# Six pairs of split-weight tiles, 13 ring tiles, and a selection made a block ahead of its gather

## The chip, the cores and the metric

One NeuronCore of a Trainium2 chip runs the whole program. The metric is the device time of one execution in microseconds (us). Engines: TensorE (PE: matmuls; PEld: its weight loads), VectorE (DVE), ScalarE (ACT), GpSimd (POOL), SyncE (SP, which issues nearly all the loads here).

## What is computed

Two layers of a decoder trunk for 256 tokens of width 1024, in float32. The change touches only the last part, the mixture of experts of the second layer; its reference is

```python
def moe_swiglu(t, router, w_gate, w_up, w_down):
    logits = (t @ router).astype(jnp.float32)
    top_logits, top_idx = lax.top_k(logits, TOP_K)          # 2 of 8 experts
    gates = jax.nn.softmax(top_logits, axis=-1)
    combine = jnp.sum(jax.nn.one_hot(top_idx, N_EXPERTS, dtype=jnp.float32) * gates[..., None], axis=1)
    out = jnp.zeros_like(t)
    for e in range(N_EXPERTS):
        out = out + combine[:, e:e + 1].astype(t.dtype) * swiglu(t, w_gate[e], w_up[e], w_down[e])
    return out
```

with `swiglu` = `(silu(t @ w_gate) * (t @ w_up)) @ w_down` and experts 3584 wide. All eight experts' weights, 352 MB, are read once. A final RMSNorm follows.

## The kernel before, in words

**Turns.** The experts are worked off in eight turns (`experts`, line 1360). After routing, the experts are ranked by their count of tokens, and `KIND` alternates a large turn ("L", up to 128 tokens) with a small one ("S", up to 64 tokens). Which expert a turn takes is known only on the chip; SP loads its number into a register (`turns`, lines 1353 to 1355) and addresses the weights with it.

**Pieces.** A turn has seven blocks of 512 hidden columns. A block has eight gate/up pieces (`gate_up`) and four down pieces (`down`); a piece is a 128 x 1024 slab of float32 weights. In program order the gate/up pieces of block fc + 1 come before the down pieces of block fc. Each piece is split into two float32r tiles, high and low (`split_to`): ScalarE copies the slab into the high part, VectorE subtracts it to get the low part, and TensorE multiplies with both. A large turn needs six matmuls per piece (the tokens are split as well), a small one four: the high and low halves of its 64 tokens stand beside each other in one 128-wide operand.

**The hidden tile.** A large turn's product of silu and up is transposed and split in `hidden_T`. A small turn's is folded from its two halves by matmuls, goes through silu, product and split in `fold`, and these steps are put off by a count of pieces (`after`, counted down by `tick` after each piece).

**The selection and the gather** (`dispatch`, line 1387). For the next turn, `pick` compares the slot numbers with the ranks on VectorE (tile `sel`, two comparisons); TensorE gathers the tokens with `sel` as an operand (tile `xT`), transposes `sel` for the later combine, and `split_to` writes the gathered tokens to the tile `x`, one buffer shared by all turns. `dispatch` is a generator, advanced twice per down piece in the fifth block (fc = 4, lines 1639 to 1643), and once per down piece in the sixth. `combine` adds a turn's output to `h` during the next turn.

**Buffers and order.** Raw weights land in a ring of 16 tiles of 1 MB (`ring`: four `wraw0`, seven `wraw2`, three pairs of `wraw`, two `a8p`). There are four pairs of split tiles (`whl`, three; `whl2`, one), and `run_ahead` (line 1482) splits `AHEAD` = 3 pieces beyond the one in use. From line 1717 on, TensorE, ScalarE and VectorE keep the order in which the program issues (`in_order`); SP's loads are ordered by the planner, each as soon as its ring tile is free. Ahead of the experts, `NRAW2` = 7 loads go to `wraw2` at once (line 1609), and one more is issued by GpSimd.

Of the kernel before, what the change touches and what calls it, by code (L numbers as in the profile page):

```python
# [11 lines left out]
F32R = mybir.dt.float32r  # L12
# [17 lines left out]
CDEC = -math.exp(-0.5)  # L30
NEG = -1.0e30
NWRAW = 6
NRAW2 = 7
NRAW0 = 4
AHEAD = 3
PRE = 2


# [72 lines left out]
def _build(tc, nc, es, I, out, dbg, upto):  # L111
# [1248 lines left out]
    def experts(kinds, late=None, hook=None):  # L1360
# [26 lines left out]
        def dispatch(e, late=None):  # L1387

            large = kinds[e] == "L"
            sel = mt.tile([128, 2, 128], F32, name="sel", bufs=1)  # L1390
            rk = col(e, 0)

            def pick(tb):
                if large:
                    nc.vector.tensor_scalar(sel[:, tb, :], iota, rk(tb), None, op0=OP.is_equal)
                else:
                    nc.vector.tensor_scalar(sel[:, tb, :].rearrange("p (a b) -> p a b", a=2),
                                            iota[:, None, 0:64].to_broadcast([128, 2, 64]), rk(tb), None,
                                            op0=OP.is_equal)

            def gather(q, k, tb):
                c = slice((4 * q + k) * 128, (4 * q + k + 1) * 128)
                nc.tensor.matmul(pts[q][:, k, :], lhsT=N.t[tb][:, c], rhs=sel[:, tb, :],
                                 start=tb == 0 and (k == 0 or late is None), stop=tb == 1 and (k == 3 or late is None))
            pts = {}

            def parts(q):
                if q == 0:
                    X[e] = mo.tile([128, 2, 8, 128], F32R, name="x")
                split_to(X[e][:, 0, 4 * q:4 * q + 4], X[e][:, 1, 4 * q:4 * q + 4], pts[q])  # L1410

            def turned():
                pt = ps([128, 2, 128], "selT")
                for tb in range(2):
                    nc.tensor.transpose(pt[:, tb, :], sel[:, tb, :], ident)
                yield
                sT = SEL[e] = mt.tile([128, 2, 128], F32R, name="sT")
                nc.scalar.copy(out=sT, in_=pt)
                yield
            pick(0)  # L1420
            if late is None:
                pick(1)
            yield
            if not large:
                pt = ps([128, 8, 64], "xT")
                for kb in range(8):
                    for tb in range(2):
                        nc.tensor.matmul(pt[:, kb, :], lhsT=N.t[tb][:, kb * 128:(kb + 1) * 128], rhs=sel[:, tb, 0:64],  # L1428
                                         start=tb == 0, stop=tb == 1)
                    if kb % 2:  # L1430
                        yield
                yield from turned()
                yield "parts"
                for _ in range(2):
                    yield
                X[e] = mo.tile([128, 2, 8, 128], F32R, name="x")[:, 0]
                split_to(X[e][:, :, 0:64], X[e][:, :, 64:128], pt)
            else:
                if late is not None:
                    next(late)  # L1440
                    for q in range(2):
                        pts[q] = ps([128, 4, 128], "xT")
                        for k in range(4):
                            gather(q, k, 0)
                            if (q, k) == (1, 1):
                                next(late)
                    pick(1)
                    next(late, None)
                for q in range(2):
                    if late is None:  # L1450
                        pts[q] = ps([128, 4, 128], "xT")
                    for k in range(4):
                        if late is None:
                            gather(q, k, 0)
                        gather(q, k, 1)
                        if k % 2:
                            yield
                    if late is not None:
                        parts(q)
                yield from turned()  # L1460
                if late is None:
                    yield "parts"
                    for q in range(2):
                        yield
                        parts(q)
# [38 lines left out]
        def gate_up(e, fc):  # L1504
            large = kinds[e] == "L"
            acc = []
            sums = {}
            for w in range(2):
                a = ps([128, 512], "gu", "gu")
                for i in range(4):  # L1510
                    wh, wl = piece()
                    terms = []
                    for k in range(2):
                        kb = 2 * i + k
                        c = slice(k * 512, (k + 1) * 512)
                        x = (X[e][:, 0, kb, :], X[e][:, 1, kb, :]) if large else X[e][:, kb, :]
                        terms.append((a, x, (wh[:, c], wl[:, c]), kb == 0, kb == 7))
                    products(large, terms)
                    tick()
                    next(side[0], None)  # L1520
                acc.append(a)
                if not large:
                    t = sums[w] = mt.tile([128, 512], F32, name=("msg", "mhl")[w], **({} if w else {"bufs": 1}))
                    after(1 if (e, fc) == (last, NFC - 1) else 3, lambda t=t, a=a: nc.scalar.copy(out=t, in_=a))
            end = (e, fc) == (last, NFC - 1)
            if not large:
                return fold(sums, end)
            sgt = mt.tile([128, 512], F32, name="msg", bufs=1)
            nc.scalar.activation(sgt, acc[0], AF.Silu)
            if end:  # L1530
                preload(AF.Sqrt)
            nc.vector.tensor_tensor(out=sgt, in0=sgt, in1=acc[1], op=OP.mult)
            return sgt

        def fold(sums, end):

            H = mt.tile([128, 4, 128], F32R, name="mhh")
            t = mt.tile([128, 512], F32, name="mhl").rearrange("p (w f t) -> p w f t", w=2, f=4)
            pt = []

            def turned(w, fs):
                if not pt:
                    pt.append(ps([128, 2, 4, 64], "hT", "hT"))
                for f in fs:
                    nc.tensor.matmul(pt[0][:, w, f, :], lhsT=sums[w][:, f * 128:(f + 1) * 128], rhs=C("fold"),  # L1545
                                     start=True, stop=True)

            def silu():
                nc.scalar.activation(t[:, 0], pt[0][:, 0], AF.Silu)

            def times():
                nc.vector.tensor_tensor(out=t[:, 1], in0=t[:, 0], in1=pt[0][:, 1], op=OP.mult)  # L1552

            def parts():
                split_to(H[:, :, 0:64], H[:, :, 64:128], t[:, 1])
            for i in range(4):
                after(2 if end else 2 + i, lambda i=i: turned(i // 2, range(2 * (i % 2), 2 * (i % 2) + 2)))
            for n, f in zip((2, 2, 2) if end else (7, 8, 10), (silu, times, parts)):
                after(n, f)
            if end:  # L1560
                after(5, lambda: preload(AF.Sqrt))
            return H
# [67 lines left out]
        for e in range(len(kinds)):  # L1630
            Y = [ps([128, 512], "Y", "Y") for _ in range(2)]
            for fc in range(NFC):
                if fc + 1 < NFC:
                    nx = gate_up(e, fc + 1)
                elif e < last:
                    nx = gate_up(e + 1, 0)
                else:
                    nx = None
                if fc == NFC - 3 and e < last:
                    nxt = dispatch(e + 1)  # L1640
                    side[0] = until_parts(nxt)
                    hd = down(e, fc, hd, Y, nx, 2)
                    run(side[0])
                elif fc == NFC - 2 and e < last:
                    side[0] = nxt
                    hd = down(e, fc, hd, Y, nx, 1)
                    run(nxt)
                else:
                    hd = down(e, fc, hd, Y, nx)
                if (e, fc) == (0, 1) and hook is not None:  # L1650
                    side[0] = hook()
            side[0] = combine(e, Y, 3 if e < last else 0)
# [4 lines left out]
    last = 99  # L1657
# [33 lines left out]
    mt = left(es, "moet", 2)  # L1691
    mo = left(es, "moe", 1)
    ring[:0] = [wraw] * (NWRAW // 2) + [a8p]
    parts_.append(left(es, "whl2", 1))
    dump("h3", h)
    if upto <= 3:
        return
# [108 lines left out]
```

## Time and profile before

| | us |
|---|---|
| median of 3 runs | 1521.27 (1520.98 to 1522.26) |
| profiled execution | 1520.23 |
| its span, first to last instruction | 1518.2 |
| TensorE matmuls busy | 1439.5 (95%) |
| VectorE busy | 1244.5 (82%) |
| ScalarE busy | 1047.0 (69%) |
| mean granted TensorE clock, share of full | 0.987 |

Busy times are summed over the whole span, and the two layers' other parts take the first 550 us or so; what an engine does in the turns has to be read from stretches within them. Matmuls are pipelined and their ends are modelled, so the time from one start to the next says more than a matmul's duration. A gather matmul of the program appears as two matmuls in the trace.

### The profile page before, as it was taken

The page shows a single profiled execution, that of the slowest core. Times are in us where ns is not written, and L with a number is a line of the kernel's source. Part 1 is how long each engine was busy: PE and PEld are TensorE (multiplying, and loading weights), DVE is VectorE, ACT ScalarE, POOL GpSimd, SP SyncE. Part 2 cuts the span into 40 slices and gives each one's busy share as a digit, 9 for nine tenths or more (in the row PEclk, how much of TensorE's full clock was granted, in tenths as well). Part 3 has the DMA queues.
Part 4 walks back from the last instruction along what each step waited for, and adds up shares of the span by engine and source line. Part 5 has one row for each costly group of instructions (what it writes and reads, how often), then busy time and mean ns, then how long its engine had stood idle before and what let it go on. Part 6 is the DMA issues. An engine that isn't in the chain of part 4 may idle for free. (4 is left out here: it accounts for less than half of the span.)

```text
span 1518.2 us, 22487 instructions
## 1 busy us (share of the span) xinstructions
PE 1439.5 (95%) x7781; PEld 1206.6 (79%) x7781; DVE 1244.5 (82%) x1634; ACT 1047.0 (69%) x1440; POOL 85.9 (6%) x154
## 2 busy tenths in 40 slices
PE   7889899999999999999989999989999989999995
PEld 6879888998888888787678887777888678878774
DVE  6786865554486669989989989989989989998996
ACT  6644345444454567879878769878768879777895
POOL 4223010001020010000000000000000000000000
PEclk9999999999999999999999999999999999999998
DMA  8230025557554659889999989999999999998961
GB/s 301 73 103 24 1 85 185 187 182 268 192 180 140 262 187 380 333 341 388 400 371 400 355 334 382 404 381 389 367 358 341 400 417 358 374 368 330 389 270 46
DMA packets 78994, 426.85 MB, mean 281 GB/s; under 512 B 9280, under 2 KB 9552, under 8 KB 43920
## 3 DMA queue, kind: packets, MB, share of 16 engines
q1 hardware_dynamic: 78048, 422.38, 73.9%
q0 software_dynamic: 816, 2.87, 0.6%
q8 instruction: 65, 1.06, 0.3%
q14 instruction: 65, 0.53, 0.1%
HBM read 424.15 MB, written 1.05 MB: 280 GB/s over the span
## 5 line engine op out<-in xcount | busy, mean ns | idle before, releaser
L193 DVE TENSOR_TENSOR wlo<-mraw,whi 128x1024 fp32r<-128x1024 f32 x546 | 645.1, 1220 | 48.3 <-ACT whi L192 39.9
L192 ACT CAST whi<-mraw 128x1024 fp32r<-128x1024 f32 x546 | 559.9, 1050 | 118.5 <-PE Y L1500 57.3
L1500 PE MATMUL gu<-whi,x 128*128 128x512 f32 x1344 | 388.1, 397 | 0.1
L193 DVE TENSOR_TENSOR wlo<-raw,whi 128x1024 fp32r<-128x1024 f32 x242 | 291.3, 1220 | 108.1 <-ACT whi L192 105.6
L192 ACT CAST whi<-raw 128x1024 fp32r<-128x1024 f32 x242 | 250.1, 1043 | 132.7 <-PE acc L197 37.9
L1500 PEld LDWEIGHTS gu<-whi,x 128*128 128x128 f32 x1344 | 248.3, 188 | 52.6 <-DVE x L193 0.4
L1502 PE MATMUL gu<-wlo,x 128*128 128x512 f32 x896 | 282.6, 397 | 3.7 <-DVE wlo L193 2.8
L1502 PEld LDWEIGHTS gu<-wlo,x 128*128 128x128 f32 x896 | 165.0, 188 | 53.3 <-DVE wlo L193 17.9
L1500 PE MATMUL Y<-whi,mhh 128*128 128x512 f32 x448 | 171.3, 422 | 18.2 <-DVE mhh L193 17.8
L1502 PE MATMUL Y<-wlo,mhh 128*128 128x512 f32 x448 | 141.9, 398 | 0.7
L1500 PEld LDWEIGHTS Y<-whi,mhh 128*128 128x128 f32 x448 | 79.2, 190 | 41.1 <-DVE mhh L193 28.7
L1502 PEld LDWEIGHTS Y<-wlo,mhh 128*128 128x128 f32 x448 | 84.0, 190 | 24.0 <-DVE wlo L193 4.9
L196 PE MATMUL cp<-u,whi 128*128 128x256 f32 (+1 forms) x360 | 101.9, 283 | 0.0
L197 PE MATMUL cp<-u,wlo 128*128 128x256 f32 (+1 forms) x360 | 101.8, 283 | 0.0
L198 PE MATMUL cp<-u,whi 128*128 128x256 f32 (+1 forms) x360 | 101.8, 283 | 0.0
L1500 PE MATMUL Y<-whi,mhl 128*128 128x512 f32 x224 | 88.0, 393 | 0.0
L197 PEld LDWEIGHTS cp<-u,wlo 128*128 128x128 f32 (+1 forms) x360 | 68.3, 190 | 0.3
L196 PEld LDWEIGHTS cp<-u,whi 128*128 128x128 f32 (+1 forms) x360 | 68.3, 190 | 0.3
L198 PEld LDWEIGHTS cp<-u,whi 128*128 128x128 f32 (+1 forms) x360 | 68.3, 190 | 0.2
L1500 PEld LDWEIGHTS Y<-whi,mhl 128*128 128x128 f32 x224 | 42.2, 188 | 7.9
L196 PE MATMUL tp<-whi,u 128*128 128x512 f32 x96 | 40.8, 425 | 2.4 <-DVE u L193 2.4
L197 PE MATMUL tp<-whi,u 128*128 128x512 f32 x96 | 39.5, 412 | 2.2 <-DVE u L193 2.2
(425 smaller groups left out, 1985.1 us busy)
## 6 DMA issues: line engine op xcount, KB each, us to landing
mraw<-in_moe SPq DMA_DIRECT2D x272, 1024.0 KB, 7.2
raw<-in_moe SPq DMA_DIRECT2D x126, 512.0 KB, 7.5
raw<-in_ffn_gu SPq DMA_DIRECT2D x44, 512.0 KB, 4.0
raw<-in_w_in SPq DMA_DIRECT2D x38, 512.0 KB, 3.9
raw<-in_ffn_d SPq DMA_DIRECT2D x22, 512.0 KB, 3.6
raw<-in_w_out SPq DMA_DIRECT2D x16, 512.0 KB, 3.6
raw<-in_w_in SPq DMA_DIRECT2D x4, 416.0 KB, 8.9
h<-in_x SPq DMA_DIRECT2D x2, 512.0 KB, 6.2
```

The source lines that it names most:

```text
L192: nc.scalar.copy(out=hi, in_=src)
L193: nc.vector.tensor_tensor(out=lo, in0=src, in1=hi.bitcast(F32), op=OP.subtract)
L196: nc.tensor.matmul(o, lhsT=a[0], rhs=b[0], start=start, stop=False)
L197: nc.tensor.matmul(o, lhsT=a[1], rhs=b[0], start=False, stop=False)
L198: nc.tensor.matmul(o, lhsT=a[0], rhs=b[1], start=False, stop=stop)
L1500: nc.tensor.matmul(o, lhsT=x, rhs=b[0], start=start and i == 0, stop=False)
L1502: nc.tensor.matmul(o, lhsT=a[0] if large else a, rhs=b[1], start=False, stop=stop)
```

## The change

Six pairs of split tiles instead of four (`whl2` has three, and stands three times in the list of pools that the splits take in turn), and `AHEAD` is 5. `wraw2` has four tiles instead of seven, so the ring has 13. A small turn's gathered tokens get a tile of their own, `xs`, of half the size. In `experts`, `dispatch` of the next turn is begun, and its selection made, right after the down pieces of the fourth block; the rest follows in the fifth as before, and its last steps (the split of the gathered tokens) run in the gate/up pieces issued next. The counts by which `fold` and the copies of a small turn's sums are put off fall by two, except in the last block.

```diff
-NRAW2 = 7
+NRAW2 = 4
 NRAW0 = 4
-AHEAD = 3
+AHEAD = 5
...
-                X[e] = mo.tile([128, 2, 8, 128], F32R, name="x")[:, 0]
+                X[e] = mo.tile([128, 8, 128], F32R, name="xs")
                 split_to(X[e][:, :, 0:64], X[e][:, :, 64:128], pt)
...
-                    after(1 if (e, fc) == (last, NFC - 1) else 3, lambda t=t, a=a: nc.scalar.copy(out=t, in_=a))
+                    after(1, lambda t=t, a=a: nc.scalar.copy(out=t, in_=a))
...
-            for n, f in zip((2, 2, 2) if end else (7, 8, 10), (silu, times, parts)):
+            for n, f in zip((2, 2, 2) if end else (5, 6, 8), (silu, times, parts)):
...
                 if fc == NFC - 3 and e < last:
-                    nxt = dispatch(e + 1)
                     side[0] = until_parts(nxt)
                     hd = down(e, fc, hd, Y, nx, 2)
                     run(side[0])
+                    if late is not None:
+                        side[0] = nxt
                 elif fc == NFC - 2 and e < last:
                     side[0] = nxt
                     hd = down(e, fc, hd, Y, nx, 1)
                     run(nxt)
                 else:
                     hd = down(e, fc, hd, Y, nx)
+                    if fc == NFC - 4 and e < last:
+                        nxt = dispatch(e + 1)
+                        next(nxt)
...
-    parts_.append(left(es, "whl2", 1))
+    parts_.extend([left(es, "whl2", AHEAD - 2)] * (AHEAD - 2))
```

## Rows read from the trace of the kernel before

The windows view gives, for a stretch (us from the start of the span), its length, the busy time of TensorE's matmuls (PE), its weight loads (PEld), VectorE (DVE), ScalarE (ACT) and GpSimd (POOL), each with its count of instructions, then the granted TensorE clock, the share of the DMA engines that was busy and the GB/s that they moved. A timeline gives the start, the time, the instructions, and in brackets the idle time before them and what ended it.

**Rows 1.** windows view, a large turn, then a small one (columns told above)

```profile
820.97:941.66 120.69, 119.57 (x558) 98.29 (x556) 110.41 (x106) 93.79 (x103) 0.00 (x0) 1.00 0.94 357
941.66:1056.60 114.94, 107.07 (x510) 85.12 (x508) 108.38 (x111) 97.30 (x119) 0.00 (x0) 0.99 0.98 391
```

**Rows 2.** timeline of VectorE in a small turn (start us, us, what, idle before)

```profile
989.88 8.03 DVE L193 TENSOR_TENSOR wlo<-mraw,whi 128x1024 fp32r<-128x1024 f32 x7
997.83 3.49 DVE L193 TENSOR_TENSOR wlo<-raw,whi 128x1024 fp32r<-128x1024 f32 x3
...
1011.06 1.23 DVE L193 TENSOR_TENSOR wlo<-mraw,whi 128x1024 fp32r<-128x1024 f32 x1 [1.88 <-ACT whi L192]
1015.40 1.23 DVE L193 TENSOR_TENSOR wlo<-mraw,whi 128x1024 fp32r<-128x1024 f32 x1 [3.11 <-ACT whi L192]
1017.90 1.23 DVE L193 TENSOR_TENSOR wlo<-mraw,whi 128x1024 fp32r<-128x1024 f32 x1 [1.27 <-ACT whi L192]
```

**Rows 3.** timeline of TensorE in the same small turn

```profile
990.01 0.72 PE L1500 MATMUL Y<-whi,mhh 128*128 128x512 f32 x2 [0.73 <-DVE mhh L193]
...
997.46 0.62 PE L1500 MATMUL gu<-whi,x 128*128 128x512 f32 x2
...
1001.14 0.62 PE L1500 MATMUL gu<-whi,x 128*128 128x512 f32 x2
...
1004.31 0.73 PE L1500 MATMUL Y<-whi,mhh 128*128 128x512 f32 x2 [0.73 <-DVE mhh L193]
...
1007.91 1.19 PE L1403 MATMUL xT<-sel,un 128*128 128x128 f32 x8 [2.40 <-DVE sel L1395]
...
1013.21 0.56 PE L1545 MATMUL hT<-csk,msg 128*128 128x64 f32 x4
1013.58 0.70 PE L1500 MATMUL Y<-whi,mhh 128*128 128x512 f32 x2
...
1014.59 1.05 PE L1403 MATMUL xT<-sel,un 128*128 128x128 f32 x8
1015.49 0.38 PE L1415 MATMUL selT<-ident,sel 128*128 128x128 f32 x2
...
1026.08 0.74 PE L1500 MATMUL Y<-whi,mhh 128*128 128x512 f32 x2 [0.58 <-DVE mhh L193]
```

**Rows 4.** waits view, 640 to 1518 us: total us, times, longest us

```profile
PE Y L1500 <- DVE mhh L193: 17.8, 24, 0.9
...
PE xT L1403 <- DVE sel L1395: 7.2, 3, 2.4
...
PE xT L1428 <- DVE sel L1397: 4.5, 4, 1.1
...
ACT whi L192 <- DMA mraw<-in_moe: 3.6, 11, 0.3
```

**Rows 5.** timeline of the last block, VectorE, then ScalarE

```profile
1489.73 4.62 DVE L193 TENSOR_TENSOR wlo<-raw,whi 128x1024 fp32r<-128x1024 f32 x4
1494.27 0.41 DVE L1552 TENSOR_TENSOR mhl<-mhl,hT 128x256 f32<-128x256 f32 x1
1495.15 0.43 DVE L193 TENSOR_TENSOR mhh<-mhl,mhh 128x256 fp32r<-128x256 f32 x1 [0.47 <-ACT mhh L192]
...
1497.24 2.35 DVE L193 TENSOR_TENSOR wlo<-mraw,whi 128x1024 fp32r<-128x1024 f32 x2
...
1500.19 1.08 ACT L192 CAST yh<-Y 128x512 fp32r<-128x512 f32 x2 [0.62 <-PE Y L1502]
```

**Rows 6.** timeline, SP's issue of raw tiles, ScalarE's first copies from them

```profile
999.07 6.68 SPq L167 DMA_DIRECT2D raw<-in_moe  x6
...
1043.60 2.94 ACT L192 CAST whi<-raw 128x1024 fp32r<-128x1024 f32 x3
```

**Rows 7.** DMA issues by line, KB each, median us to landing

```profile
raw<-in_moe SPq DMA_DIRECT2D x126, 512.0 KB, 7.5
```

**Rows 8.** windows view, 25 us inside a small turn

```profile
750.00:775.00 25.00, 20.84 (x95) 15.87 (x95) 23.53 (x26) 20.21 (x25) 0.00 (x0) 0.97 1.01 419
```

## The prediction

> **What bounds the kernel now.** I read the busy time of each engine by expert turn first. From the first combine of one turn to that of the next, a large turn takes 120.69 us and TensorE is busy for 119.57 of them: TensorE is the bound. A small turn takes 114.94 us, TensorE is busy for 107.07 and VectorE for 108.38 [rows 1]. Who bounds a small turn shows on the two timelines. VectorE's low parts follow each other without a gap, seven in 997.83 - 989.88 = 7.95 us, so 1.136 us from one to the next [rows 2]. TensorE does four gate/up pieces in 1001.14 - 997.46 = 3.68 us, 0.92 each, and a block comes every 1004.31 - 990.01 = 14.30 us, with a wait for the hidden tile in each [rows 3]. Twelve low parts are 13.63 us, and the two hidden operations fill the rest of 14.30: there VectorE is the bound and TensorE's waits are its slack. So the kernel alternates: TensorE's time in large turns, VectorE's in small ones, and the split pairs are all that one can carry over to the other.
>
> The third thing to see is where this alternation breaks: the block of a small turn in which the next large turn's tokens are gathered. TensorE stands 2.40 us for the selection, then does 8 gather matmuls, one piece and 16 gather matmuls in 1013.21 - 1007.91 = 5.30 us, and waits again, 0.58 us, for the next hidden tile [rows 3]. VectorE, the bound, idles 1.88 + 3.11 + 1.27 = 6.26 us in the same block, because every pair is full [rows 2]. The waits by pair of instructions give the counts: 3 selections of 2.4 us in small turns, 4 of 1.1 us in large ones, 4.5 us together, 24 waits for a hidden tile, and for the weight loads only 3.6 us in 11 pieces of at most 0.3 [rows 4].
>
> **The change part by part.**
>
> *The selection a block ahead.* Its two comparisons are issued after the down pieces of the fourth block instead of between those of the fifth, so twelve pieces stand between them and the gather; VectorE does the same two, and its queue holds nothing else that has to move for them. No load is issued by this step, so neither SP's queue nor POOL's is passed. In the three small turns that gather a large one, the 2.40 us go. After that wait the stretch of 5.30 us ran slow: 8 gather matmuls later take 1015.49 - 1014.59 = 0.90 us [rows 3], so 24 of them and a piece of about 1.0 should take 3.7; 1.6 us are lost to the standing before it, and the granted clock, 1.00 over the large turn, is 0.99 over the small one [rows 1]. Between nothing and 1.6 I take 1.6, because the later rows of the same block are at full rate. The 0.58 us go too, since they follow from VectorE's idle time. That is 2.40 + 1.6 + 0.58 = 4.6 us a turn, 13.7 in three. The upper end is VectorE's own idle time there, 6.26 a turn, 5.0 more in three; the lower end is 2.40 alone, 6.5 less. In the four large turns TensorE is the bound, and their 4.5 us go whole [rows 4].
>
> *Six pairs, five pieces ahead.* A large turn leaves VectorE idle for 120.69 - 110.41 = 10.3 us [rows 1], enough to make two more pieces. Each small turn then starts with two more in hand: 2 x 1.136 = 2.27 us in which TensorE needn't wait, 9.1 in four turns. From below nothing (if ScalarE's copies ahead of them don't get through), from above 9.1; I take 9.1, since in large turns both engines already run at the limit that the pairs set. After the gather block TensorE will have been busy with gathers for some 4 us, in which VectorE gets over three pieces ahead; with three pairs of lead it stopped, with five it should go on.
>
> The Trainium skill bears on this ("Perfetto Trace Analysis", Optimization Strategy): a gap that repeats on the engine that ought to be saturated can mean too few buffers. By that the 24 waits for a hidden tile would all go and the time would be that of the last rival, 1462; by the row on VectorE, which has no gap in those blocks, they stay whatever the buffers, and the sum is the one below.
>
> *The hidden steps' counts.* They fall by two where the split runs two further ahead (10 + 3 = 8 + 5 for the last step), so on VectorE and ScalarE each stands behind the same piece as before. Nothing, while VectorE is the bound.
>
> *The last block* keeps its counts of 2, so its hidden chain now stands behind two more splits. Before: four low parts, the two hidden steps at 1494.27 and 1495.15, then three low parts until 1499.59, and the combine begins at 1500.19 [rows 5]. After: six low parts, to 1489.73 + 6 x 1.136 = 1496.55; the hidden steps, 1.3 us as in those rows, to 1497.9 or, with the last write, 1498.2; then TensorE still has four pieces of 0.92, to 1501.9. This costs 1.7 us, at most twice that, at least nothing.
>
> *The tile of the 64 tokens.* Its copy and its low part (and the two of a large turn) move from the down pieces into the gate/up pieces before; they are as many as before, and what they read is complete by then. The transposed selection is copied one piece earlier, behind its matmul; ScalarE stands for part of a piece there and the splits behind it wait, covered by the five pieces in hand. Nothing; without that cover 0.9 us in seven turns.
>
> *Thirteen ring tiles.* The three loads fewer ahead of the experts are issued later, by SP's same queue. A raw tile issued at 999.07 is first read at 1043.60, 44.5 us later [rows 6], and lands in 7.5 [rows 7]. With 13 of 16 tiles the distance is 36 us, 29 more than the landing needs. Nothing. If that cover went, each tile would cost the 1.048 MB that it is short: at the pair's mean of 374 GB/s [rows 1], 2.8 us each, 8.4 in all.
>
> *Sum.* 13.7 + 4.5 + 9.1 - 1.7 = 25.6 us. The profiled execution took 1520.23 us (span 1518.2), so 1494.6; it lies 1.04 under the median of 1521.27, which makes **1495.7 us**.
>
> **The rivals.**
>
> *The stream becomes the bound (slower).* A small turn moves 391 GB/s x 114.94 us = 44.9 MB; 6.9 us shorter, it would need 416 GB/s. For it: that is as high as the best stretch of 25 us, 419 [rows 8], and the ring is shorter. Against it: the copies hardly ever wait for a load [rows 4], and even at 391 GB/s the shortfall of a turn would be 2.7 MB of a ring of 13. If the stream could hold only the pair's mean of 374 GB/s, it would be the bound from the start, nothing of the gain would show, and the three tiles fewer would cost 8.4 us beside the 1.7 of the last block: 1531.4. It decides where the distance between issue and use falls to the 7.5 us of a landing. The Trainium skill gives this rule ("DMA: Bandwidth & Descriptors", Where 436 GB/s comes from): for loads from HBM the memory side binds, at about 358 GB/s a core (the page has faster single transfers while the pair's other core is idle). By that rule the stream is past its limit already and no small turn can shorten; the trace disagrees, with 391 over a whole turn.
>
> *The wait for the selection was free (no change).* Small turns are VectorE's, and a TensorE wait there may only take up slack; with no lead from the pairs either, 4.5 - 1.7 = 2.8 us are left: 1518.5. Against it: VectorE's own 6.26 us of idle time in that block.
>
> *The two extra pairs carry nothing:* 9.1 us less, 1504.8. For it: one in-order ScalarE copies for all pieces and can hold the low parts back.
>
> *The selection doesn't move on the chip:* the order of loads is left to the planner. Against it: VectorE is held to the order in which the program issues. Then 9.1 - 1.7 = 7.4 us are left: 1513.9.
>
> *Every repeated gap goes.* A block of a small turn is twelve pieces of 0.92 and four transposes of the hidden tile of 0.37 (1013.58 - 1013.21 [rows 3]), 12.5 us of TensorE's work in 14.30; 24 x 1.8 = 43 us in place of 9.1, 1462. It needs VectorE to be faster than its rows.
>
> **How the numbers follow.** The forecast has 0.69, the pairs that carry nothing 0.11, the selection that stays 0.05, the free wait 0.06, the stream 0.07, the gaps that go 0.02. The forecast's own bounds are 1495.7 - 5.0 - 1.7 = 1489 and, with the clock's 4.8 and the 1.7 a second time, about 1502; the case without a lead reaches 1504.8, and with the low end of the gather block 1511. So 1489 to 1511 leaves out at most 0.2. Over 0.2%, 3 us, is about what a measurement of this kernel can tell from no change. Faster: 0.69 + 0.11 + 0.05 + 0.02 = 0.87; the same 0.06; slower 0.07.
>
> **What would show it.** Right: no wait of a gather matmul for a selection; VectorE idle under 2 us in the gather block of a small turn; the pair of turns some 8 us shorter than 235.6, about 7 of it in the small one; the clock at 1.00 throughout; the combine at the end 1.7 us later against the last low part. Waits of copies for weight loads of more than a few tenths would speak for the stream. A small turn shortened by 4.6 alone would say that the pairs carry nothing. I am wrong if the small turn keeps its 115 us or if the large one grows.

## The result, and the profile after

| | before | after |
|---|---|---|
| median, us | 1521.12 (4 runs, 1519.63 to 1522.26) | 1499.05 (4 runs, 1497.61 to 1502.07) |
| profiled execution, us | 1520.23 | 1500.03 |
| its span, us | 1518.2 | 1498.2 |
| mean granted TensorE clock | 0.987 | 0.989 |

The ratio is 0.9858 with a 95% interval of 0.9839 to 0.9877: 22.1 us faster by the medians, where 25.6 were forecast. The predicted 1495.7 is 3.4 us too low, and the measured time lies within the range.

**Turns.** The windows view of the changed kernel, from first combine to first combine: a large turn, the small turn after it, and the last small turn up to its combine (columns as in [rows 1]).

```profile
815.86:934.98 119.12, 119.12 (x558) 98.52 (x556) 109.46 (x106) 92.91 (x103) 0.00 (x0) 1.00 0.96 371
934.98:1044.29 109.31, 104.45 (x509) 83.97 (x508) 107.76 (x111) 95.90 (x119) 0.00 (x0) 1.00 1.01 404
1391.88:1479.80 87.92, 80.03 (x381) 62.87 (x379) 84.25 (x87) 75.10 (x95) 0.00 (x0) 1.00 0.70 274
```

Against [rows 1] the small turn went from 114.94 to 109.31 and the large one from 120.69 to 119.12. The pair is 235.63 - 228.43 = 7.2 us shorter, 5.6 of it in the small turn; 8.0 were forecast, about 7 of it there. TensorE is now busy through all of a large turn. In a small turn VectorE is idle for 109.31 - 107.76 = 1.55 us instead of 114.94 - 108.38 = 6.56. The last small turn took 87.91 before (the same stretch, 1412.92 to 1500.83) and takes 87.92 now: it gained nothing.

**The gather block.** VectorE's timeline in that small turn, to hold against [rows 2]:

```profile
1005.25 2.36 DVE L193 TENSOR_TENSOR wlo<-mraw,whi 128x1024 fp32r<-128x1024 f32 x2 [0.78 <-ACT whi L192]
1008.38 1.23 DVE L193 TENSOR_TENSOR wlo<-mraw,whi 128x1024 fp32r<-128x1024 f32 x1 [0.78 <-ACT whi L192]
```

and TensorE's, to hold against [rows 3]:

```profile
997.61 1.95 PE L1403 MATMUL xT<-sel,un 128*128 128x128 f32 x16
...
1000.31 1.95 PE L1403 MATMUL xT<-sel,un 128*128 128x128 f32 x16
...
1013.80 0.74 PE L1500 MATMUL Y<-whi,mhh 128*128 128x512 f32 x2 [0.32 <-DVE mhh L193]
```

No gather matmul waits for its selection, the two groups of 16 run at a granted clock of 1.00, and VectorE idles 1.56 us in the block, where it had idled 6.26. Its two gaps of 0.78 us follow two stands of ScalarE, which makes its high parts (ScalarE's timeline): one for the transposed selection, one for the folding transposes ahead of silu.

```profile
1003.89 0.38 ACT L1418 CAST sT<-selT 128x256 fp32r<-128x256 f32 x1 [1.95 <-PE selT L1415]
...
1007.03 0.38 ACT L1549 ACTIVATE mhl<-hT 128x256 f32<-128x256 f32 x1 [0.87 <-PE hT L1545]
```

**The waits**, 640 to 1498 us (pair of instructions, us in total, times, longest us), answering to [rows 4]:

```profile
ACT mhh L192 <- DVE mhl L1552: 29.5, 21, 2.5
...
ACT sT L1418 <- PE selT L1415: 17.1, 7, 2.8
ACT mhl L1549 <- PE hT L1545: 15.1, 16, 1.2
...
PE Y L1500 <- DVE mhh L193: 12.1, 17, 1.5
DVE wlo L193 <- PE Y L1500: 11.6, 4, 2.9
...
PE Y L1500 <- DVE yl L193: 4.8, 4, 1.2
```

Both waits for a selection are gone from this list, and so is every wait of a copy for a weight load. Of TensorE's 24 waits for a hidden tile 17 are left. Three lines are new, or nearly so, and weren't foreseen in this size: ScalarE stands 16 times, 15.1 us in all, for the folding transposes ahead of silu (`mhl <- hT`, once and 1.8 us before); it stands for the transposed selection (3 times, 1.6 us before); and TensorE waits 4 times, once a small turn, for the low half of the combine's operand (`yl`). The first and the third are tried by themselves below; the second was not. VectorE's four waits of up to 2.9 us for TensorE fall in the gather blocks of the large turns, where VectorE has time to spare. That ScalarE waits longer for VectorE's product (`mhh <- mhl`, 12.0 us before) was not followed up.

**The end.** The changed kernel's last block on VectorE, then TensorE, then ScalarE; [rows 5] are the same block before.

```profile
1467.20 3.53 DVE L193 TENSOR_TENSOR wlo<-mraw,whi 128x1024 fp32r<-128x1024 f32 x3
1470.60 3.53 DVE L193 TENSOR_TENSOR wlo<-raw,whi 128x1024 fp32r<-128x1024 f32 x3
1474.01 0.46 DVE L1552 TENSOR_TENSOR mhl<-mhl,hT 128x256 f32<-128x256 f32 x1
1474.93 0.43 DVE L193 TENSOR_TENSOR mhh<-mhl,mhh 128x256 fp32r<-128x256 f32 x1 [0.47 <-ACT mhh L192]
1475.88 1.23 DVE L193 TENSOR_TENSOR wlo<-raw,whi 128x1024 fp32r<-128x1024 f32 x1 [0.52 <-ACT whi L192]
```

```profile
1475.41 0.73 PE L1500 MATMUL Y<-whi,mhh 128*128 128x512 f32 x2 [1.50 <-DVE mhh L193]
```

```profile
1479.16 1.07 ACT L192 CAST yh<-Y 128x512 fp32r<-128x512 f32 x2 [1.71 <-PE Y L1502]
```

As forecast, six low parts now run ahead of the last hidden step, and TensorE stands 1.50 us for it. The combine begins 1479.16 - 1477.11 = 2.05 us after the last low part, where it had been 0.60: 1.45 us, against 1.7 forecast.

**The first turn** has a wait that I hadn't looked for. TensorE's timeline, before and then after:

```profile
626.70 0.66 PE L1567 MATMUL hT<-ident,msg 128*128 128x128 f32 x4 [0.55 <-DVE msg L1532]
```

```profile
628.76 0.66 PE L1567 MATMUL hT<-ident,msg 128*128 128x128 f32 x4 [2.36 <-DVE msg L1532]
```

In the first turn VectorE also does the routing, one step with every piece, and the product of silu and up now stands behind two more splits with their routing steps: 1.8 us more.

### The profile page after: what moved, and what is told of

It is laid out like the page before. It is cut to its first block, busy times and chain, and to the rows that moved or that the text cites. A ratio compares the mean times of both kernels' runs of the same rounds, so it can differ in the third digit from the quotient of the medians.

```text
span 1498.2 us, 22516 instructions
## 1 busy us (share of the span) xinstructions
PE 1428.0 (95%) x7781; PEld 1206.2 (81%) x7781; DVE 1238.6 (83%) x1634; ACT 1038.0 (69%) x1440; POOL 85.9 (6%) x154
## 4 chain that ended last, share of the span: by engine, by line
PE 80%; DVE 11%; issue 3%; ACT 3%; DMA 2%; POOL 1%; SPq 0%; DVEq 0%; ACTq 0%
PE gu L1500 17%; PE gu L1502 10%; PE Y L1500 10%; PE Y L1502 6%; DVE wlo L193 5%; PE cp L197 4%; PE cp L198 4%; PE cp L196 4%; PE hT L1545 2%; PE acc L197 2%; PE acc L196 2%; PE acc L198 2%; PE tp L197 2%; PE tp L198 2%; PE tp L196 2%
## 5 line engine op out<-in xcount | busy, mean ns | idle before, releaser
L193 DVE TENSOR_TENSOR wlo<-raw,whi 128x1024 fp32r<-128x1024 f32 (+1 forms) x270 | 323.5, 1228 | 106.8 <-ACT whi L192 99.8
L192 ACT CAST whi<-raw 128x1024 fp32r<-128x1024 f32 (+1 forms) x270 | 276.5, 1043 | 120.6 <-PE acc L197 37.9
L1500 PE MATMUL gu<-whi,x 128*128 128x512 f32 x896 | 244.1, 394 | 0.6 <-ACT msg L1529 0.5
L1500 PEld LDWEIGHTS gu<-whi,x 128*128 128x128 f32 x896 | 167.7, 188 | 37.6 <-ACT msg L1529 0.9
L1500 PE MATMUL Y<-whi,mhh 128*128 128x512 f32 x448 | 168.9, 416 | 16.9 <-DVE mhh L193 12.1
L1502 PE MATMUL gu<-wlo,xs 128*128 128x512 f32 x448 | 142.5, 399 | 2.9 <-DVE wlo L193 2.9
L1500 PE MATMUL gu<-whi,xs 128*128 128x512 f32 x448 | 143.7, 402 | 0.0
L1502 PE MATMUL gu<-wlo,x 128*128 128x512 f32 x448 | 138.4, 390 | 0.0
L1502 PEld LDWEIGHTS gu<-wlo,xs 128*128 128x128 f32 x448 | 81.7, 188 | 30.9 <-DVE wlo L193 14.5
L1502 PEld LDWEIGHTS gu<-wlo,x 128*128 128x128 f32 x448 | 84.2, 188 | 19.2
L1500 PEld LDWEIGHTS gu<-whi,xs 128*128 128x128 f32 x448 | 80.7, 189 | 14.6
```

The lines of the kernel that those rows point to most:

```text
L192: nc.scalar.copy(out=hi, in_=src)
L193: nc.vector.tensor_tensor(out=lo, in0=src, in1=hi.bitcast(F32), op=OP.subtract)
L1500: nc.tensor.matmul(o, lhsT=x, rhs=b[0], start=start and i == 0, stop=False)
L1502: nc.tensor.matmul(o, lhsT=a[0] if large else a, rhs=b[1], start=False, stop=stop)
```

## The experiments

Theory: the selection made sooner is worth most of the gain, the two more pairs carry the rest over from the large turns to the small ones. Main rivals: the wait for the selection was free; the pairs carry nothing; the load stream bounds. Each run is compared with runs of the kernel before on the same chip (medians of 1520.8 to 1521.1).

### One half of the change at a time

The kernel before with the selection made a block ahead, four pairs and 16 ring tiles as they were:

```diff
                 if fc == NFC - 3 and e < last:
-                    nxt = dispatch(e + 1)
...
+                    if fc == NFC - 4 and e < last:
+                        nxt = dispatch(e + 1)
+                        next(nxt)
```

> The kernel before with nothing but the selection made a block ahead: four pairs, 16 ring tiles, the old counts. If the selection acts as forecast, the waits of gather matmuls for a selection (7.2 + 4.5 us) go, and the slow stretch behind them: 3 x (2.4 + 1.6) + 4.5 = 16.5 us less, about 1504.5 us; VectorE's idle time in the gather block shrinks but stays above 2 us, since three pieces of lead are too few to bridge 4 us of gathers. If the wait was free because small turns are VectorE's, only the 4.5 us of the large turns go: about 1516.5 us. If the gain of the change is that of the pairs, no change: 1521 us.

Measured: 1504.71 us, ratio 0.9893 (0.9877 to 0.991), 16.1 us faster. The windows view of this kernel, a large turn and a small one:

```profile
816.59:935.95 119.36, 119.36 (x557) 98.36 (x556) 109.91 (x106) 93.53 (x103) 0.00 (x0) 1.00 0.95 363
935.95:1047.38 111.43, 105.69 (x509) 83.61 (x508) 107.96 (x111) 97.14 (x119) 0.00 (x0) 1.00 1.01 403
```

The small turn is 3.5 us shorter than in [rows 1] and the large one 1.3. VectorE's idle time in the small turn is 111.43 - 107.96 = 3.47 instead of 6.56, and nearly all of it is one gap, in the gather block. ScalarE, in the order in which it is given its work, stands there for the transposed selection before it makes the next high part, and VectorE waits for that (timelines of VectorE, then ScalarE):

```profile
1008.17 5.77 DVE L193 TENSOR_TENSOR wlo<-mraw,whi 128x1024 fp32r<-128x1024 f32 x5 [3.39 <-ACT whi L192]
```

```profile
1006.33 0.37 ACT L1418 CAST sT<-selT 128x256 fp32r<-128x256 f32 x1 [2.81 <-PE selT L1415]
```

How much of the 3.39 us is this stand and how much the full pairs was not separated.

So the wait for the selection was not free. But the turn shrank by what VectorE's idle time shrank, 3.1 us, and by 0.4 us that its instructions took less; the forecast had taken 4.6 us off TensorE's waits. TensorE's timeline shows which of these went. The wait of 2.40 us is gone, and from the first gather to the transposed selection TensorE takes 1005.91 - 1000.02 = 5.89 us instead of 1015.49 - 1007.91 = 7.58 [rows 3]. The wait for the next hidden tile, 0.58 us before, is still there:

```profile
1000.02 1.95 PE L1403 MATMUL xT<-sel,un 128*128 128x128 f32 x16
...
1005.91 0.38 PE L1415 MATMUL selT<-ident,sel 128*128 128x128 f32 x2
...
1016.93 0.73 PE L1500 MATMUL Y<-whi,mhh 128*128 128x512 f32 x2 [0.73 <-DVE mhh L193]
```

The other half, the changed kernel with the selection back in the fifth block:

```diff
                 if fc == NFC - 3 and e < last:
+                    nxt = dispatch(e + 1)
...
-                    if fc == NFC - 4 and e < last:
-                        nxt = dispatch(e + 1)
-                        next(nxt)
```

> The changed kernel with the selection back between the down pieces of the fifth block: six pairs, five ahead, 13 ring tiles, the new counts. If the pairs carry what the last small turn of the changed kernel shows (it lost 1.45 us at its end and came out level, so 1.45 us a turn), 4 x 1.45 - 1.45 = 4.4 us less from that, and up to 2.3 us in each of three gather blocks where VectorE can go on for two more pieces while TensorE stands: 1510 to 1517 us. If they carry nothing, the last block's 1.5 us more: about 1522.5 us. If the two parts only work together, the sum of this gain and that of the selection alone is well below the 22 us of the change.

Measured: 1522.76 us, ratio 1.0015 (1.0006 to 1.0025): no gain at all, 1.9 us slower, so that the gain I had expected of the pairs did not come. TensorE's timeline and the waits view say why:

```profile
1009.52 2.08 PE L1403 MATMUL xT<-sel,un 128*128 128x128 f32 x8 [4.68 <-DVE sel L1395]
```

```profile
PE xT L1403 <- DVE sel L1395: 14.0, 3, 4.7
PE Y L1500 <- DVE mhh L193: 12.0, 17, 1.5
...
PE Y L1500 <- DVE yl L193: 4.8, 4, 1.2
```

VectorE takes its work in order. With five pieces ahead the selection stands behind two more splits, 2 x 1.136 = 2.27 us, and the wait for it grows from 2.40 to 4.68, that is by 2.28. The lead that two more pairs give is spent again: waits for a hidden tile fall from 17.8 to 12.0 us [rows 4] (1.50 of them the new wait in the last block), but the wait for the selection rises from 7.2 to 14.0, and 4.8 us for `yl` are new. The two halves of the change are not independent terms: the pairs are worth nothing until the selection is out of their way.

### The ring

The kernel before with 13 tiles, and the changed kernel with 10:

```diff
-NRAW2 = 7
+NRAW2 = 4
```

> The kernel before with 13 ring tiles in place of 16, nothing else. If loads land far ahead of their use, no change: 1521 us within 3, and the distance from issue to first copy falls from 44.5 to about 36 us. If the stream bounds the kernel, the three tiles fewer cost up to 8.4 us: about 1529 us, with waits of copies for loads of over 1 us.

```diff
-NRAW2 = 4
+NRAW2 = 1
```

> The changed kernel with 10 ring tiles in place of 13. If loads land far ahead of their use, no change: 1499 us within 2, with the distance from issue to first copy at about 10/13 of that with 13. If the stream is near its limit in the shorter small turns, waits of copies for loads of several us and more than 1505 us.

Measured: 1520.52 us, 0.9999 (0.9989 to 1.0008), and 1498.97 us, 0.9862 (0.9845 to 0.9879): no change in either. The small turn of the kernel with 10 tiles, in the windows view, moves 404 GB/s like that of the changed one:

```profile
933.33:1042.66 109.33, 104.45 (x509) 83.91 (x509) 107.75 (x111) 95.93 (x119) 0.00 (x0) 1.00 1.01 404
```

The stream is not the bound, with three or with six tiles fewer. The distance from issue to first copy shrinks as expected: a raw tile issued at 989.29 is copied at 1024.80 in the kernel before with 13 tiles, 35.5 us; one issued at 989.35 is copied at 1013.16 in the changed kernel with 10, 23.8 us. With 10 tiles a few small waits for loads show, 1.3 us at most, where the changed kernel has none (the kernel before has some, of 1.9 us at most); they cost nothing.

### The new waits of the changed kernel

The combine's count of 3 isn't lowered with the others, so `yl` stands behind two more splits. With the count at 1:

```diff
-            side[0] = combine(e, Y, 3 if e < last else 0)
+            side[0] = combine(e, Y, 1 if e < last else 0)
```

> The changed kernel with the combine of a turn begun two pieces sooner (its count of 3 was left as it was, so its low parts stand behind two more splits, and TensorE waits 0.4 + 1.2 us for them in each small turn). If VectorE bounds the small turn there, these waits are slack: they go, and the time stays at 1499 us within 2. If they are on the path, 4 x 1.6 = 6.4 us less: about 1492.7 us.

Measured: 1499.31 us, 0.9858 (0.9842 to 0.9874), no change. The waits for `yl` are gone from the turns, and those for the hidden tile are longer by about as much (waits view; 12.1 in 17 in the changed kernel):

```profile
PE Y L1500 <- DVE mhh L193: 17.7, 21, 1.5
```

It was slack: in a small turn TensorE waits for VectorE at one place or at another.

ScalarE's new wait for the folding transposes need not be slack, because ScalarE feeds VectorE. With those transposes asked for one piece sooner:

```diff
-                after(2 if end else 2 + i, lambda i=i: turned(i // 2, range(2 * (i % 2), 2 * (i % 2) + 2)))
+                after(2 if end else 1 + i, lambda i=i: turned(i // 2, range(2 * (i % 2), 2 * (i % 2) + 2)))
```

> The changed kernel with the four folding transposes of a small turn's hidden tile one piece sooner each (the last block as it was). In the changed kernel ScalarE, now up to five pieces ahead, stands 1.2 us before the silu for these transposes in 16 of the blocks, and cannot copy meanwhile. If that is what keeps the lead of two pieces at 1.45 us a turn in place of 2.27, about 4 x 0.8 = 3 us less: 1496 us. If the standing is slack, no change: 1499 us within 1.5.

Measured: 1495.77 us, 0.984 (0.9827 to 0.9854), 3.3 us under the changed kernel's median. The 16 waits of silu are one of 0.2 us. The small turn (windows view) is 1.0 us shorter, and VectorE idles 1.23 us in it:

```profile
932.10:1040.38 108.28, 104.13 (x510) 83.92 (x508) 107.05 (x110) 95.39 (x118) 0.00 (x0) 1.00 1.01 408
```

The changed kernel moved silu two pieces sooner, but not the transposes that silu reads; ScalarE stood at that point, its copies behind it stood too, and that took part of the lead.

The first turn, with the routing's steps spread, one step with every second piece instead of every one:

```diff
-                    side[0] = hook()
+                    side[0] = (None for _ in hook() for _ in range(2))
```

> The changed kernel with the routing steps of the first turn, which VectorE does one after each of eight pieces, done one after every second of sixteen. In the changed kernel TensorE waits 2.36 us for the product of silu and up behind them, where it was 0.55 before. If that wait is on the path (the first turn is TensorE's), 1.8 us less or a little more: about 1497 us. If TensorE makes it up later in the turn, no change: 1499 us.

Measured: 1496.78 us, 0.984 (0.9827 to 0.9853), 2.3 us under the changed kernel's median. The wait of 2.36 us is gone, and TensorE is busy throughout that turn from 583 us on.

### The counts

The changed kernel with the counts of before (3 for the copies, 7, 8 and 10 for the folding steps):

```diff
-                    after(1, lambda t=t, a=a: nc.scalar.copy(out=t, in_=a))
+                    after(1 if (e, fc) == (last, NFC - 1) else 3, lambda t=t, a=a: nc.scalar.copy(out=t, in_=a))
...
-            for n, f in zip((2, 2, 2) if end else (5, 6, 8), (silu, times, parts)):
+            for n, f in zip((2, 2, 2) if end else (7, 8, 10), (silu, times, parts)):
```

> The changed kernel with the old counts of the hidden steps (3; 7, 8, 10), so that each stands behind two more splits. If VectorE bounds the small turns, TensorE waits longer for each hidden tile, by two low parts (2.3 us) at most, with two pieces ready behind it, and the time stays near 1499 us, at most 3 us up. If the hidden tile is on the path, 24 blocks of up to 2.3 us: as far as 1550 us.

Measured: 1509.36 us, 0.9919 (0.9905 to 0.9932): 10.3 us slower than the changed kernel, where I had expected 3 at most. TensorE's timeline after the gather block, and the waits view:

```profile
1021.72 0.73 PE L1500 MATMUL Y<-whi,mhh 128*128 128x512 f32 x2 [2.21 <-DVE mhh L193]
```

```profile
PE Y L1500 <- DVE mhh L193: 32.4, 24, 2.2
```

Uncorrected, the hidden steps stand behind two more low parts, and each small turn is 112.9 to 113.5 us long. TensorE stands longer for the hidden tile, VectorE fills its pairs meanwhile and then idles 3.39 us in the gather block, as in the kernel with the selection alone and behind the same stand of ScalarE, 2.81 us. So the lower counts belong to the gain: without them the lead is spent on waiting for the hidden tile.

### The last block

A first attempt to hold the split back at the end to three pieces ahead:

```diff
-            run_ahead()
+            run_ahead(4 if len(units) == 0 and len(raws) + len(ready) <= 12 else 1 + AHEAD)
```

> The changed kernel with the split held to three pieces ahead for the last twelve pieces, so that the last hidden chain stands behind the same pieces as in the kernel before. If the last block's cost is as forecast, the 1.5 us that TensorE waits for the last hidden tile go: about 1497.5 us, and the combine begins 0.6 us after the last low part, not 2.05. If the lead is worth more there than the order, slower by up to 2.3 us: 1501 us.

Measured: 1499.88 us, 0.9861 (0.9846 to 0.9876). The condition came true too late and changed no engine's order, so this is a repeat of the changed kernel and tells nothing of the end. With a condition that comes true in time:

```diff
-            run_ahead()
+            run_ahead(4 if 2 * len(units) + len(raws) + len(ready) <= 12 else 1 + AHEAD)
```

> The changed kernel with the split held to three pieces ahead for the last twelve pieces, now counted over all that are left to use, so that VectorE does the last hidden steps behind four low parts and three follow them, as in the kernel before. If the last block's cost is as forecast, the wait of 1.50 us for the last hidden tile goes and the combine begins about 0.6 us after the last low part in place of 2.05: 1.5 us less, about 1497.5 us. If TensorE only waits elsewhere, 1499 us.

Measured: 1496.49 us, 0.9846 (0.9832 to 0.9859), 2.6 us under the changed kernel's median. On VectorE four low parts stand ahead of the last hidden step instead of six, and on ScalarE the combine's copy is back to 0.6 us after the last low part (timelines of VectorE, then ScalarE):

```profile
1469.70 0.40 DVE L1552 TENSOR_TENSOR mhl<-mhl,hT 128x256 f32<-128x256 f32 x1
1470.57 0.43 DVE L193 TENSOR_TENSOR mhh<-mhl,mhh 128x256 fp32r<-128x256 f32 x1 [0.47 <-ACT mhh L192]
1471.52 3.50 DVE L193 TENSOR_TENSOR wlo<-raw,whi 128x1024 fp32r<-128x1024 f32 x3 [0.52 <-ACT whi L192]
```

```profile
1475.61 1.07 ACT L192 CAST yh<-Y 128x512 fp32r<-128x512 f32 x2 [0.62 <-PE Y L1502]
```

Within one execution, from the last turn's first combine to the end's, this is 86.45 us against 87.92, so 1.47; the rest of the 2.6 is what medians of a few runs differ by.

### The three repairs together

The transposes sooner, the routing spread and the last block held back, on the changed kernel.

> The changed kernel with three edits together: the folding transposes one piece sooner, the routing steps spread over sixteen pieces, and the split held to three ahead for the last twelve pieces. If the three places are apart and each lies on the path, 3.3 + 2.3 + 1.5 = 7.1 us less than the changed kernel: about 1492 us. If they take up each other's slack, the best of them alone: 1496 us.

Measured: 1491.24 us (5 runs, 1489.6 to 1492.63), ratio 0.9808 (0.9794 to 0.9821). It beats both kernels: 29.8 us under the one before and 7.8 under the changed one, about the sum of the three edits by themselves (3.3 + 2.3 + 2.6 = 8.2). In the windows view, a small turn and the last one:

```profile
929.86:1038.10 108.24, 104.12 (x510) 83.95 (x508) 107.00 (x110) 95.38 (x118) 0.00 (x0) 1.00 1.00 407
1384.57:1470.38 85.81, 80.28 (x382) 62.56 (x380) 83.60 (x86) 74.71 (x94) 0.00 (x0) 1.00 0.70 282
```

What is left of VectorE's idle time in that small turn is one gap, and it follows ScalarE's stand for the transposed selection (timelines of ScalarE, then VectorE):

```profile
998.58 0.37 ACT L1418 CAST sT<-selT 128x256 fp32r<-128x256 f32 x1 [2.41 <-PE selT L1415]
```

```profile
999.93 3.50 DVE L193 TENSOR_TENSOR wlo<-mraw,whi 128x1024 fp32r<-128x1024 f32 x3 [1.24 <-ACT whi L192]
```

This is the step that no run moved. In three small turns it would be worth 3 x 1.24 = 3.7 us at most, which is an estimate.

The medians of the changed kernel and of three that ought to equal it (its repeat, 10 tiles, combine sooner) differ by 0.9 us, which is not small against gains of 2 to 3. The stretch of the experts within one execution is steadier: from the first gate/up matmul to the first combine matmul at the end. These are its two ends on TensorE's timeline, before and then after:

```profile
563.00 1.51 PE L1500 MATMUL gu<-whi,x 128*128 128x512 f32 x4
...
1500.83 0.49 PE L1602 MATMUL cmb<-yh,sT 128*128 128x512 f32 x1 [0.45 <-ACT yh L192]
```

```profile
564.24 1.50 PE L1500 MATMUL gu<-whi,x 128*128 128x512 f32 x4
...
1479.80 0.50 PE L1602 MATMUL cmb<-yh,sT 128*128 128x512 f32 x1 [0.44 <-ACT yh L192]
```

| kernel | this stretch, us |
|---|---|
| before | 937.8 |
| before, 13 ring tiles | 937.3 |
| selection alone | 922.0 |
| pairs alone | 940.2 |
| changed; its repeat; 10 tiles; combine sooner | 915.6; 915.5; 915.6; 915.4 |
| changed, counts of before | 926.6 |
| changed, transposes sooner | 911.8 |
| changed, routing spread | 913.3 |
| changed, last block held | 914.0 |
| changed, all three | 907.8 |

By it the change gains 22.3 us, and the three edits 3.8, 2.3 and 1.6, which is 7.7, as much as the three together.

## Why the prediction was right, and where its sizes were off

The sign and the range held, and in the main the mechanism; the forecast gain was 3.5 us too large. By its steps, with the turns of the profiled executions (the first turn from its first gate/up matmul to the first combine):

| step of the sum | forecast, us | measured, us | from |
|---|---|---|---|
| selection, three small turns | 13.7 | 10.5 | 3 x (114.94 - 111.43), selection alone |
| selection, four large turns | 4.5 | 5.3 | 3 x (120.69 - 119.36), and the first turn: 706.00 - 563.00 before, 705.13 - 563.48 with the selection alone |
| two more pieces, four small turns | 9.1 | 7.8 | 3 x (111.43 - 109.31), and 87.90 - 86.45 in the last, from the runs with the selection alone and with the last block held |
| two more pieces, large turns | 0 | 0.7 | 3 x (119.36 - 119.12) |
| first turn, routing | not seen | -0.6 | 705.13 - 563.48 with the selection alone, 706.53 - 564.24 after |
| last block | -1.7 | -1.45 | 2.05 - 0.60 |
| sum | 25.6 | 22.3 | 22.1 by the medians |

The routing by itself costs more than the 0.6 us that the first turn lost: with its steps spread that turn goes from 142.3 to 703.69 - 563.68 = 140.0.

**The selection in the small turns** is the term that was mis-sized most. I added three waits of TensorE (2.40 + 1.6 + 0.58) in turns of which I had just said that VectorE bounds them. What a small turn gains is what VectorE no longer idles, and with four pairs 3.39 us of its idle time in the gather block stay. The wait of 2.40 and the 1.6 us of slow matmuls (1.7 measured) were there and are gone; the 0.58 us did not go, TensorE stands 0.73 there. Twelve pieces between the selection and the gather were a miscount that did no harm: the program has nine, and eight low parts stand between them in the small turn shown with the selection alone, six in the changed kernel. The rival by which the wait for the selection was free falls: by itself the selection gave 16.1 us.

**The two more pieces** were forecast at 2.27 us a small turn and gave 2.12 in three of them and 1.45 in the last. Their bound from below, "if ScalarE's copies ahead of them don't get through", was partly met: ScalarE stands 1.2 us at silu, and with the transposes one piece sooner a small turn gains another 1.0. The forecast had put the term into the sum beside the selection's, as if either half could be had alone. That is wrong: the pairs alone gave nothing. The rival by which they carry nothing is right without the selection and false with it, and the one by which the selection stays in place, priced at 7.4 us of gain, would have come out at 1.9 of loss.

**The first turn** is a step that the prediction lacked: it let every count be made good for the deeper split, and the routing's steps, one for every piece, were not.

**The last block** was right in mechanism and size; it cancels the last turn's lead, which is why that turn's 87.9 us didn't move.

**The counts** at nothing: right for the counts as changed; the run with those of before shows that 10 us hang on them.

**The tile of the 64 tokens and the ring** at nothing: the ring is shown, by two runs. The tile wasn't tried by itself. The transposed selection was to hold ScalarE for part of a piece, covered by the pairs in hand. That step failed: ScalarE stands 2.8 us at most, 17.1 in seven turns, and the cover doesn't hold in the small turns, where VectorE idles 0.78 us behind it in the changed kernel and 1.24 with the three repairs. It hardly differs from the 19.7 us of the kernel with the selection alone, so the deeper split doesn't bring it. What moving it would give wasn't measured.

**The stream** falls. The distance between issue and first copy did shrink more than I had worked out (a raw tile issued at 981.52 is copied at 1012.83, so 31.3 us instead of 36), still four landings of 7.6 us. The rule that I set beside this rival, the Trainium skill's "DMA: Bandwidth & Descriptors", Where 436 GB/s comes from, with some 358 GB/s for loads from HBM, does not agree with this case: the small turn moves 404 GB/s over 109 us, and 408 in the kernel with the transposes sooner. The page has that figure as one core's half of what two cores share. Here one core runs the program, and no run loads from both.

**Every repeated gap goes** falls too: in a steady block TensorE still stands 0.73 us for the hidden tile (17 waits are left in all), with VectorE busy throughout. Here the trace sides against the reading of the Trainium skill's "Perfetto Trace Analysis", Optimization Strategy, that such a gap can mean too few buffers: six pairs in place of four, by themselves, took 5.8 us off these gaps and put 6.8 on the selection's.

What stays open: executions of one kernel differ by 1.4 to 5.6 us. In the profile after, the code ahead of the experts, where the change only issues three loads fewer, ended 1.24 us later than before (564.24; the other profiles with 13 tiles have 562.3 to 564.5), and the code behind the end's first combine matmul, which the change leaves as it was, took 18.45 us instead of 17.37 (17.1 to 18.8 in the other profiles). Where that comes from was not traced. More than six pairs weren't tried: the copies' count is at 1 and can hardly be lowered again to make up for them.

## What to carry to other kernels

On an engine that works in order, a deeper look-ahead moves every small step that another engine waits for behind that much more bulk work. Go through all of them (selections, counts put off by pieces, routing steps, the last block) and move each with the depth, and what it reads too; here the look-ahead alone was worth -1.9 us, with the selection out of its way 5.7 more than the selection alone, and with three more steps moved another 7.8. One step, the copy of the transposed selection, was left standing in the way. Price a removed wait by the idle time of the engine that bounds the stage, not by the length of the wait on the engine that stood.

## What the runs showed of the hardware that was not expected

The granted clock fell at the long waits of TensorE. Windows of TensorE's stretch just after the wait: the kernel before (after 2.40 us of standing), then the changed kernel with the selection back in the fifth block (after 4.68 us).

```profile
1007.90:1010.50 2.60, 2.59 (x12) 2.30 (x13) 1.28 (x2) 0.51 (x1) 0.00 (x0) 0.69 1.02 408
1010.50:1013.20 2.70, 2.70 (x17) 2.60 (x17) 1.23 (x1) 1.02 (x2) 0.00 (x0) 0.66 1.06 417
```

```profile
1009.50:1012.00 2.50, 2.48 (x10) 2.38 (x11) 1.30 (x2) 0.00 (x0) 0.00 (x0) 0.50 1.02 423
1012.00:1014.60 2.60, 2.60 (x20) 2.42 (x19) 1.03 (x1) 1.05 (x1) 0.00 (x0) 0.91 1.00 413
```

0.50 is the lower of the two levels (1.2 of 2.4 GHz), and 0.69 and 0.66 are means over both. After the waits of 0.73 us in the steady blocks no such dip shows, and in the changed kernel's turns the granted clock is 1.00 throughout. With the counts undone, the wait of 2.21 us shown above was followed by 1.00 and another of 2.00 us, at 958.32, by 0.64 from there to 963 us, so the length of one wait alone does not tell the clock after it.

The second is the load stream: all 16 DMA engines are busy through a small turn (share 1.01) at 404 GB/s, and with 10 ring tiles too nothing waits on it that counts. I had left a chance to a stream that holds only the pair's 374 GB/s; no run here shows where it ends.
